# Attention's second score product and the mLSTM's g product over 128 partitions in place of 64

## The chip, the core and the metric

The kernel runs on one core of a Trainium2 chip. The metric is device time in microseconds (us) of one execution. The core has TensorE (PE, with its weight loader PEld), VectorE (DVE), ScalarE (ACT) and GpSimd (POOL), which take their instructions in an order of their own each and wait for each other by semaphores; SyncE (SP) issues the DMAs.

## What is computed

Two layers, each of a mixer and a feed-forward block, on 512 tokens of 1024 features, with a norm ahead of and behind each block. The mixer has eight heads of dilated attention (64 features each) and four heads of an mLSTM (128 features each, two directions, chunks of 128 tokens):

```python
def reference(x, ...):
    for l in range(DEPTH):                       # 2
        mixed = hybrid_mixer(rms_norm(x, mix_pre_g[l]), w_in[l], ..., w_out[l])
        x = x + rms_norm(mixed, mix_post_g[l])
        ff = conv_ffn(rms_norm(x, ffn_pre_g[l]), w_up[l], ..., w_down[l])
        x = x + rms_norm(ff, ffn_post_g[l])
...
        # one step of a direction of the mLSTM, for one chunk
        inter = bcum + m_st[..., None]
        m_t = jnp.maximum(inter, jnp.max(dlog, axis=-1))
        sc = jnp.einsum('bhte,bhse->bhts', qc, kc) * jnp.exp(dlog - m_t[..., None])
        g = jnp.exp(inter - m_t)
        num = jnp.einsum('bhts,bhsf->bhtf', sc, vc) + g[..., None] * jnp.einsum('bhte,bhef->bhtf', qc, c_st)
```

## The kernel before

Activations lie in SBUF with the feature on the partition and the 512 tokens along the row. Each float32 operand of a projection is split into a high and a low part, and a product is made of three: high by high, low weight by high, high weight by low (`mac`, L200 to L202). The weights come in 192 pieces of at most 512 KB over SP's queue into three raw buffers; ACT makes the high part of a piece (L153) and DVE the low part (L91).

In the mixer the projections run through PE in a written order, and the side work of the heads is put between them: `Stream` A steps through the generators `attn`, and `Stream` M through `gates` and `mlstm`, a step after so many tiles of products. A planner then fixes the order of each engine's instructions when the program is made, by priorities, by the costs that it assumes and by the points that `issue_after` sets. Work of the norms is due after a certain number of rows of products (`later`, `settle`).

*Attention scores.* `rot_out` turns the queries and keys of two heads, a and b, in one tile of 128 partitions (a in rows 0 to 63, b in rows 64 to 127). Of the queries it makes one tile per head, with the head's high part in its own 64 rows and the low part in the other 64. Of the keys it makes one tile per head with the high part twice (`ak0`, `ak1`), and one tile `ak2` with the low parts of both heads. In `scores` L710 makes low and high query by high key in one product over 128 partitions, and L711 adds high query by low key, over the head's own 64 partitions. DVE then adds a bias and takes the minimum (L716), ACT makes the exponentials (L719) and scales them (L721), `turn` transposes on PE (L727) and makes two parts (L730 on ACT, L91 on DVE), and L753 multiplies by the values. There are 32 score tiles in a layer.

*The mLSTM.* `gates` makes `bdm` and `bdg`, rows that hold -M and m_prev - M of a chunk as high and low parts in partitions 0 to 63, and in `bdm` also an indicator of the chunk in partitions 64 to 127. `uu` holds ones in partitions 0 to 63 and the parts of u in 64 to 127; `lu` is `uu` with the rows of other heads and directions set to nothing. L812 multiplies `lu` by `bdm` over 128 partitions, L820 multiplies the first 64 rows of `lu` by those of `bdg`; ACT makes the exponential of each (L814, L822). There are eight products of either line in a layer.

Buffers come from pools by tag; a new tile on a tag waits until the readers of the last one are through. The mixer's pool and the feed-forward block's lie over the same space, one after the other.

Of the kernel before, what the change touches and what calls it, by code (L numbers as in the profile page):

```python
# [9 lines left out]
F32R = mybir.dt.float32r  # L10
# [4 lines left out]
PSUM = bass.MemoryType.PSUM  # L15

P = 128
T = 512
D = 1024
KT = D // P  # L20
# [12 lines left out]
# per head: the order of its projections (mLSTM q and k, both values, attention q and k), and its attention's rate  # L33
# [3 lines left out]
# columns of the per-feature parameter array  # L37
# [8 lines left out]
# columns of the constant array  # L46
# [12 lines left out]
def tile_hybrid_block(ctx: ExitStack, tc: tile.TileContext, xt, w_in, w_g, w_out, w_up, w_down, par, cst, out):  # L59
    nc = tc.nc  # L60
# [77 lines left out]
    def split_w(alloc=None):  # L138
        """the next piece as exact high and low parts; alloc gives their place, n of the eight rows at a time."""
        if not raw_q:  # L140
            return None
        raw, nk = raw_q.popleft()
        parts = {}
        n = 8
        k = 0
        while k < nk:
            if alloc is None:
                hi = whi_p.tile([P, 8, P], F32R, tag="whi", name="whi")
                lo = wlo_p.tile([P, 8, P], F32R, tag="wlo", name="wlo")
            else:  # L150
                hi, lo, n = alloc()
            m = min(n, nk - k)
            nc.scalar.copy(out=hi[:, 0:m, :], in_=raw[:, k:k + m, :])  # L153
            lo_part(lo[:, 0:m, :], raw[:, k:k + m, :], hi[:, 0:m, :])
            for j in range(m):
                parts[k + j] = (hi[:, j, :], lo[:, j, :])
            parts["all"] = (hi, lo)
            k += m
        load_raw()
        return parts  # L160
# [18 lines left out]
    # work to be put into the program once the tensor engine has so many more rows of products before it  # L179
# [12 lines left out]
    def mac(ps, w, kk, rhs, first, last, cols=None):  # L192
        """ps += w[:, kk, :]^T rhs with both operands as exact high and low parts."""
        settle()
        clock[0] += 3 * (T if cols is None else cols.stop - cols.start)
        hi, lo = w[kk]
        rh, rl = rhs
        if cols is not None:
            rh, rl = rh[:, cols], rl[:, cols]
        nc.tensor.matmul(out=ps, lhsT=hi, rhs=rh, start=first, stop=False)  # L200
        nc.tensor.matmul(out=ps, lhsT=lo, rhs=rh, start=False, stop=False)  # L201
        clock[1] = nc.tensor.matmul(out=ps, lhsT=hi, rhs=rl, start=False, stop=last).ins  # L202

# [1 line left out]
    class Stream:  # L205
        """generators one after another, a step at a time behind the products that come before it."""
# [29 lines left out]
    def rsqrt(ms, n):  # L236
        """1/sqrt(ms) on [P, n], by a first guess from the exponent and Newton steps."""
        y = sm.tile([P, n], F32, tag=f"rs_y{n}", name="rs_y")
        a = sm.tile([P, n], F32, tag=f"rs_a{n}", name="rs_a")
        yi = y[:, :].bitcast(I32)  # L240
        nc.vector.tensor_scalar(yi, ms.bitcast(I32), -0.5, float(0x5F3759DF), op0=ALU.mult, op1=ALU.add)
        for _ in range(3):
            nc.vector.tensor_tensor(out=a, in0=y, in1=y, op=ALU.mult)
            nc.vector.scalar_tensor_tensor(out=a, in0=a, scalar=-0.5, in1=ms, op0=ALU.mult, op1=ALU.mult)
            nc.vector.scalar_tensor_tensor(out=y, in0=a, scalar=1.5, in1=y, op0=ALU.add, op1=ALU.mult)
        return y

    def rsqrt_cols(ms):
        """for the two columns of ms [P, 2]: RS / sqrt(ms), by a first guess from the exponent and Newton steps."""
# [9 lines left out]
        # a third-order step, a = y^2 ms within 7% of 1: (a^2 + C1 a + C0) y = s / sqrt(ms)  # L259
# [4 lines left out]
        # Newton's: (y^2 ms - 3 s^2) y = -2 s^3 / sqrt(ms)  # L264
# [7 lines left out]
    class Stats:  # L272
        """Sums of squares over the features: the first tiles add up beside the tensor engine, which sums over the
        partitions of that sum and of each of the last `own` tiles."""
# [7 lines left out]
        def add(self, src, n, hf):  # L282
            """the n-th of the KT tiles, for the tokens of one half or (None) both."""
# [17 lines left out]
        def flush(self, h):  # L301
            """what has come for a half until now, the sum of the first tiles ahead."""
            if self.sp[h] is None:
                self.sp[h] = t_ps()
                nc.vector.memset(self.sp[h][:, 0:2], EPS)
                self.sums(h, 1, self.acc[:, halves[h]])
            for g, n, sq in self.late:
                if g == h:
                    self.sums(h, n - KT + self.own + 2, sq)
            self.late = [e for e in self.late if e[0] != h]  # L310
# [6 lines left out]
        def rstd(self, hf):  # L317
            """[P, 2] for a half, a token per partition."""
# [6 lines left out]
    def row_of(r):  # L325
        """[P, 2] with a token per partition -> [P, 256] PSUM with the token along the row, in every partition."""
# [11 lines left out]
    def pre_operand(g, k, ops, st, hf):  # L338
        """x * g as parts, and the square of x into the statistics."""
        parts_of(g, k, ops, hf)  # L340
        st.add(x[k][:, slice(0, T) if hf is None else halves[hf]], k, hf)
# [29 lines left out]
    class Post:  # L371
        """x += norm(m) * g for each half of the tokens, and the next block's operand from the new x."""
# [9 lines left out]
        def put(self, k, src, cols=slice(0, T)):  # L382
            """an output tile times the norm's gain."""
# [30 lines left out]
    def first_group(ws, pss, xp, scale, extra=None):  # L414
        """the tiles whose operand is still being made: by halves of the tokens, all tiles beside each other."""
# [10 lines left out]
    def last_tiles(ws, kts, act, post, n0, also=None):  # L426
        """the last output tiles by halves of the tokens, so that the norm of the first half overlaps the second."""
# [18 lines left out]
    def mixer_first(l, xp, sp, G, more, whole=False):  # L446
# [12 lines left out]
        if whole:  # L459
            # the input comes tile by tile  # L460
# [20 lines left out]
    def mixer(l, xp, first, mp, post):  # L481
# [10 lines left out]
        # what picks a direction's and head's own rows for the decay products: the chunk's m and, below, the chunk  # L492
# [18 lines left out]
        def gates(ps):  # L511
# [14 lines left out]
            # index: direction, step, head; the backward direction's step j is chunk 3 - j  # L526
# [6 lines left out]
            # log sigmoid(f) = min(f, 0) - log1p(exp(-|f|)), the log1p as 2 atanh(e / (2 + e))  # L533
# [32 lines left out]
            # running maxima, forward for the first 16 rows and backward for the others  # L566
# [19 lines left out]
            # the state's maximum before each step, and with the step's own  # L586
# [16 lines left out]
            # keys are twice their value until here, and carry the scale  # L603
# [3 lines left out]
            # rows: -M and m_prev - M in the chunk's own columns, as parts  # L607
# [8 lines left out]
            bdg = mp.tile([P, 4, P], F32R, tag="bdg", name="bdg")  # L616
            for bd, src, place in ((bdm, nm, "Q0"), (bdg, gm, "Q1")):
# [12 lines left out]
        def conv_out(ps, i, name):  # L630
            """five taps, then twice the silu."""
# [15 lines left out]
        def v_out(pss):  # L647
            """values of both kinds with the token on partitions: [P, chunk, kind, feature], two chunks in a bank."""
# [22 lines left out]
        def rot_out(ps, name):  # L671
# [12 lines left out]
            if name == "aq":  # L684
                # a head's high and low parts on top of each other
# [3 lines left out]
            else:  # L689
                # a head's high part twice, and the low parts of both heads  # L690
                lo = mp.tile([P, T], F32R, tag="ak2", name="ak2")
                nc.scalar.copy(out=t[0][B_], in_=f32v(t[0][A_]))
                nc.scalar.copy(out=t[1][A_], in_=f32v(t[1][B_]))
                lo_part(lo[A_], a[A_], t[0][A_])
                lo_part(lo[B_], a[B_], t[1][B_])
                st[name] = (t, lo)
# [5 lines left out]
        def attn(hp):  # L702
# [3 lines left out]
            def scores(a, qt):  # L706
                r = slice(64 * a, 64 * a + 64)
# [3 lines left out]
                nc.tensor.matmul(out=s, lhsT=qs2[a][r, qs], rhs=kl[r, :], start=False, stop=True)  # L711
                p_ = mp.tile([P, T], F32, tag="p", bufs=2, name="p")
                mx = sm.tile([P, 1], F32, tag="mx", bufs=4, name="mx")
                # -(s + bias) / 8 and its minimum
# [46 lines left out]
        def mlstm(h):  # L761
# [3 lines left out]
            # keys with the token on partitions, times what enters the state  # L765
# [32 lines left out]
            # the part that each direction sees  # L798
# [8 lines left out]
            for d in range(2):  # L807
# [7 lines left out]
                # the masked half may overflow, and is nothing in sm_  # L815
# [4 lines left out]
                nc.tensor.matmul(out=gp_, lhsT=lu[0:64, :], rhs=st["bdg"][0:64].rearrange("p c t -> p (c t)"), start=True, stop=True)  # L820
# [38 lines left out]
        # projections; side work of the heads goes between them  # L859
# [3 lines left out]
        # streams of side work, each with its steps for each part of a projection tile  # L863
# [15 lines left out]
        def proj_v():  # L879
            """the tokens as the output's rows: both kinds of values beside each other."""  # L880
# [49 lines left out]
        # output projection  # L930
# [179 lines left out]
    # loads in the order in which the first products need them  # L1110
# [42 lines left out]
def _constants():  # L1153
# [32 lines left out]
    # how many of the dilated patterns hold key - query, as a bias before the scale  # L1186
# [63 lines left out]
```

## Time and profile before

| | |
|---|---|
| time, median of 3 runs | 1391.45 us (1390.81 to 1391.57) |
| span of the profiled execution | 1389.7 us; what lies around it has no record of its own, and the median stands 1.75 us above it |
| PE busy | 1359.0 us, 98%, 7152 products |
| PEld busy | 1126.2 us, 81% |
| DVE busy | 955.7 us, 69% |
| ACT busy | 721.8 us, 52% |
| POOL busy | 105.9 us, 8% |
| DMA | 115.34 MB, 83 GB/s |

A line such as L711 is a line of the kernel. In a shape, `64*128 64x512` is a left operand of 64 partitions by 128 columns and a right one of 64 by 512. PE's products overlap: the end of one is modelled, and a busy share near 1 says that some product was always under way, not how many were finished. A view of the timeline gives the start and the duration of each; one of windows gives the busy time of each engine in a stretch, the number of instructions, PE's granted clock (1.00 is 2.4 GHz, half of that is 1.2) and the DMAs' share and rate.

### The profile page before, as it was taken

The numbers are of one execution on the slowest core, as the hardware profiler recorded it, in microseconds if no ns is written. First come the engines' busy times: TensorE is split into PE (matmuls) and PEld (weight loads), VectorE is DVE, ScalarE is ACT, GpSimd is POOL, SyncE is SP. The second block draws the span as 40 slices with busy tenths as digits, with TensorE's granted clock in tenths as the row PEclk, the third lists the DMA queues.
The fourth block names the chain that finished last, engine by engine and source line by source line (L and its number), as shares of the span: only waits on it lengthen the run. The fifth ranks groups of instructions, "written<-read, shape, count | busy, mean of one in ns | idle before, by whom it ended". The sixth has DMA issues, their size and how long they took to land. (4 is left out here: it accounts for less than half of the span.)

```text
span 1389.7 us, 18680 instructions
## 1 busy us (share of the span) xinstructions
PE 1359.0 (98%) x7152; PEld 1126.2 (81%) x7152; DVE 955.7 (69%) x1885; ACT 721.8 (52%) x1226; POOL 105.9 (8%) x110
## 2 busy tenths in 40 slices
PE   7999999999999999999999999999999999999997
PEld 6778878789888888888986888787898888888886
DVE  6989788747887777422498887778479777773233
ACT  5686686754544444323356766866546444442230
POOL 0000000024000000000120000000240000000102
PEclk9999999999999999999999999999999999999999
DMA  6212122140333333233311121122412333323221
GB/s 231 61 35 88 31 61 77 48 150 2 100 98 107 91 95 99 86 96 103 99 67 61 61 61 51 42 77 74 124 47 76 107 91 96 102 87 99 90 89 61
DMA packets 34089, 115.34 MB, mean 83 GB/s; under 512 B 3664, under 2 KB 6352, under 8 KB 34000
## 3 DMA queue, kind: packets, MB, share of 16 engines
q1 hardware_dynamic: 34000, 114.15, 27.0%
q8 instruction: 56, 0.92, 0.3%
q14 instruction: 33, 0.27, 0.1%
HBM read 112.04 MB, written 2.10 MB: 82 GB/s over the span
## 5 line engine op out<-in xcount | busy, mean ns | idle before, releaser
L91 DVE TENSOR_TENSOR wlo<-wraw,whi 128x1024 fp32r<-128x1024 f32 (+1 forms) x192 | 236.5, 1234 | 180.6 <-ACT whi L153 178.8
L200 PE MATMUL mm<-ah,whi 128*128 128x512 f32 (+1 forms) x880 | 342.0, 389 | 0.0
L201 PE MATMUL mm<-ah,wlo 128*128 128x512 f32 (+1 forms) x880 | 335.3, 381 | 0.0
L202 PE MATMUL mm<-al,whi 128*128 128x512 f32 (+1 forms) x880 | 334.1, 381 | 0.9 <-DVE al L348 0.8
L153 ACT CAST whi<-wraw 128x1024 fp32r<-128x1024 f32 (+1 forms) x192 | 197.6, 1034 | 168.6 <-PE mm L202 112.4
L200 PEld LDWEIGHTS mm<-ah,whi 128*128 128x128 f32 x880 | 166.5, 189 | 39.1 <-issue 12.0
L202 PEld LDWEIGHTS mm<-al,whi 128*128 128x128 f32 x880 | 166.2, 189 | 32.3 <-issue 1.9
L201 PEld LDWEIGHTS mm<-ah,wlo 128*128 128x128 f32 x880 | 166.6, 189 | 27.8 <-issue 1.9
L296 POOL TENSOR_TENSOR acc<-acc,sq 128x512 f32<-128x512 f32 x22 | 29.6, 1345 | 764.1 <-ACT sq L293 759.8
L200 PE MATMUL mm<-hh,whi 128*128 128x512 f32 x220 | 86.7, 394 | 0.0
L201 PE MATMUL mm<-hh,wlo 128*128 128x512 f32 x220 | 86.7, 394 | 0.0
L202 PE MATMUL mm<-hl,whi 128*128 128x512 f32 x220 | 86.7, 394 | 0.0
L1029 DVE TENSOR_TENSOR u<-mm,prow 128x512 f32<-128x512 f32 x64 | 43.8, 686 | 50.1 <-PE mm L202 39.6
L893 PE MATMUL mm<-whi,ah 128*128 128x256 f32 x256 | 74.4, 292 | 0.2 <-DVE cu L633 0.2
L1046 ACT CAST hh<-cv 128x512 fp32r<-128x512 f32 x44 | 27.3, 620 | 87.5 <-DVE cv L1043 87.5
L895 PE MATMUL mm<-whi,al 128*128 128x256 f32 x256 | 72.4, 283 | 0.0
L894 PE MATMUL mm<-wlo,ah 128*128 128x256 f32 x256 | 72.4, 283 | 0.0
L1041 ACT ACTIVATE cg<-cg 128x512 f32<-128x512 f32 x44 | 27.9, 633 | 74.5 <-DVE cg L1035 74.2
L201 PE MATMUL o<-ah,wlo 128*128 128x512 f32 (+1 forms) x160 | 60.6, 379 | 0.0
L200 PE MATMUL o<-ah,whi 128*128 128x512 f32 (+1 forms) x160 | 60.5, 378 | 0.0
L202 PE MATMUL o<-al,whi 128*128 128x512 f32 (+1 forms) x160 | 60.5, 378 | 0.0
L719 ACT ACTIVATE p<-p,mx 128x512 f32<-128x512 f32 x64 | 46.1, 720 | 21.6 <-DVE mx L716 21.6
(317 smaller groups left out, 2788.3 us busy)
## 6 DMA issues: line engine op xcount, KB each, us to landing
wraw<-in_w_up SPq DMA_DIRECT2D x88, 512.0 KB, 3.6
wraw<-in_w_in SPq DMA_DIRECT2D x56, 512.0 KB, 3.5
wraw<-in_w_down SPq DMA_DIRECT2D x32, 512.0 KB, 3.5
wraw<-in_w_out SPq DMA_DIRECT2D x16, 512.0 KB, 3.5
wraw<-in_w_down SPq DMA_DIRECT2D x16, 384.0 KB, 3.1
x<-in_xt SPq DMA_DIRECT2D x4, 512.0 KB, 7.3
out_dram<-x SPq DMA_DIRECT2D x8, 256.0 KB, 2.2
tb<-in_cst SPq DMA_DIRECT2D x2, 967.0 KB, 5.1
```

The costliest lines, as they stand in the source:

```text
L91: nc.vector.tensor_tensor(out=dst, in0=src, in1=f32v(hi), op=ALU.subtract)
L153: nc.scalar.copy(out=hi[:, 0:m, :], in_=raw[:, k:k + m, :])
L200: nc.tensor.matmul(out=ps, lhsT=hi, rhs=rh, start=first, stop=False)
L201: nc.tensor.matmul(out=ps, lhsT=lo, rhs=rh, start=False, stop=False)
L202: clock[1] = nc.tensor.matmul(out=ps, lhsT=hi, rhs=rl, start=False, stop=last).ins
L296: e.tensor_tensor(out=self.acc[:, cols], in0=self.acc[:, cols], in1=sq, op=ALU.add)
L719: nc.scalar.activation(out=p_, in_=p_, func=AF.Exp, scale=-1.0, bias=mx, accum_out=den)
L893: nc.tensor.matmul(out=o_, lhsT=xh, rhs=hi, start=(k == 0), stop=False)
L894: nc.tensor.matmul(out=o_, lhsT=xh, rhs=lo, start=False, stop=False)
L895: clock[1] = nc.tensor.matmul(out=o_, lhsT=xl, rhs=hi, start=False, stop=(k == KT - 1)).ins
L1029: nc.vector.tensor_tensor(out=u, in0=ps, in1=st["row"], op=ALU.mult)
L1041: nc.scalar.activation(out=g, in_=g, func=AF.Gelu_apprx_tanh)
```

## The change

The second score product takes all 128 rows of the query's tile, and a key tile of its own for each head, `klo[0]` or `klo[1]`, which holds the low part in the head's own rows and zeros in the other 64. The zeros are written once in a layer by two memsets on POOL, and the two tiles live as long as the mixer. `bdg` gets zeros in partitions 64 to 127 by a memset on POOL, and L820 takes all 128 rows of `lu` and `bdg`. The space that the program keeps free for DMA descriptors is set to 1024 bytes of a partition. Apart from this the diff takes out comments and docstrings, and leaves their lines empty.

```diff
@@ gates
             bdg = mp.tile([P, 4, P], F32R, tag="bdg", name="bdg")
+            nc.gpsimd.memset(f32v(bdg[64:128]), 0.0)
@@ rot_out
-                lo = mp.tile([P, T], F32R, tag="ak2", name="ak2")
                 nc.scalar.copy(out=t[0][B_], in_=f32v(t[0][A_]))
                 nc.scalar.copy(out=t[1][A_], in_=f32v(t[1][B_]))
-                lo_part(lo[A_], a[A_], t[0][A_])
-                lo_part(lo[B_], a[B_], t[1][B_])
-                st[name] = (t, lo)
+                lo_part(klo[0][A_], a[A_], t[0][A_])
+                lo_part(klo[1][B_], a[B_], t[1][B_])
+                st[name] = (t, klo)
+
+        klo = [mp.tile([P, T], F32R, name=f"klo{i}") for i in range(2)]
+        nc.gpsimd.memset(f32v(klo[0][64:128]), 0.0)
+        nc.gpsimd.memset(f32v(klo[1][0:64]), 0.0)
@@ attn, scores
-                r = slice(64 * a, 64 * a + 64)
                 qs = slice(qt * P, (qt + 1) * P)
                 s = s_ps()
                 nc.tensor.matmul(out=s, lhsT=qs2[a][:, qs], rhs=kh[a], start=True, stop=False)
-                nc.tensor.matmul(out=s, lhsT=qs2[a][r, qs], rhs=kl[r, :], start=False, stop=True)
+                nc.tensor.matmul(out=s, lhsT=qs2[a][:, qs], rhs=kl[a], start=False, stop=True)
@@ mlstm
-                nc.tensor.matmul(out=gp_, lhsT=lu[0:64, :], rhs=st["bdg"][0:64].rearrange("p c t -> p (c t)"), start=True, stop=True)
+                nc.tensor.matmul(out=gp_, lhsT=lu, rhs=st["bdg"].rearrange("p c t -> p (c t)"), start=True, stop=True)
@@ kernel
-    nc = bacc.Bacc("TRN2", target_bir_lowering=False, num_devices=1)
+    nc = bacc.Bacc("TRN2", target_bir_lowering=False, num_devices=1, dynamic_dma_scratch_size=1024)
```

## Rows read from the trace of the kernel before

**Rows 1.** The page: each engine's busy time, share of the span, instructions.

```profile
PE 1359.0 (98%) x7152; PEld 1126.2 (81%) x7152; DVE 955.7 (69%) x1885; ACT 721.8 (52%) x1226; POOL 105.9 (8%) x110
```

**Rows 2.** Windows of the first mixer: length, engines' busy time (instructions), clock, DMA.

```profile
60.00:100.00 40.00, 39.31 (x195) 28.84 (x195) 33.90 (x88) 32.90 (x65) 0.00 (x0) 1.00 0.14 40
100.00:140.00 40.00, 40.00 (x260) 34.27 (x259) 37.03 (x81) 26.95 (x52) 2.90 (x2) 1.00 0.27 80
140.00:180.00 40.00, 39.64 (x241) 33.30 (x241) 31.42 (x79) 25.44 (x52) 3.44 (x2) 1.00 0.13 40
180.00:220.00 40.00, 39.13 (x215) 30.18 (x214) 32.91 (x87) 35.16 (x70) 0.00 (x0) 1.00 0.18 52
220.00:265.00 45.00, 45.00 (x253) 35.44 (x252) 35.02 (x73) 29.91 (x57) 2.59 (x2) 1.00 0.23 68
```

**Rows 3.** Groups by line and shape: count, busy us, mean ns, idle before.

```profile
L711 PE MATMUL s<-ak,aq 64*128 64x512 f32 x64 | 31.7, 495 | 0.0
...
L820 PE MATMUL s<-bdg,lu 64*128 64x512 f32 x16 | 8.0, 498 | 0.0
...
L812 PE MATMUL s<-bdm,lu 128*128 128x512 f32 x16 | 6.5, 406 | 0.0
```

**Rows 4.** Timeline of PE around one second score product: start, duration, instruction.

```profile
202.91 0.39 PE L202 MATMUL mm<-al,whi 128*128 128x512 f32 x1
203.14 0.40 PE L710 MATMUL s<-ak,aq 128*128 128x512 f32 x1
203.46 0.50 PE L711 MATMUL s<-ak,aq 64*128 64x512 f32 x1
203.89 0.50 PE L200 MATMUL mm<-ah,whi 128*128 128x512 f32 x1
204.23 0.28 PE L753 MATMUL o<-ptl,vs 128*128 128x256 f32 x1
```

**Rows 5.** Chain that ended last, second mixer: start, us on the chain, instruction.

```profile
869.83 0.43 PE s L711
...
890.83 0.23 PE s L710
891.07 0.43 PE s L711
891.49 0.43 PE mm L200
...
892.98 0.69 DVE p L716
...
950.44 0.42 PE s L711
```

**Rows 6.** Waits of PE's weight loader: what for, us in all, times, longest.

```profile
PEld s L711 <- issue: 18.3, 64, 0.4
```

**Rows 7.** Windows of L711's products alone: length, PE busy (count), clock, DMA.

```profile
60.00:100.00 40.00, 3.96 (x8) 1.00 0.14 40
100.00:140.00 40.00, 2.48 (x5) 1.00 0.27 80
140.00:180.00 40.00, 1.48 (x3) 1.00 0.13 40
180.00:220.00 40.00, 3.97 (x8) 1.00 0.18 52
220.00:265.00 45.00, 3.96 (x8) 1.00 0.23 68
```

**Rows 8.** Window of L820's products alone in the first mixer.

```profile
60.00:265.00 205.00, 3.98 (x8) 1.00 0.19 56
```

**Rows 9.** Groups of POOL by line and shape: a memset.

```profile
L104 POOL MEMSET ones<- 128x128 f32 x1 | 0.2, 204 | 0.3 <-POOLq L1237 0.3
```

**Rows 10.** Windows at the border of the two layers, columns as in rows 2.

```profile
690.00:700.00 10.00, 7.79 (x62) 6.74 (x61) 9.70 (x24) 5.37 (x14) 6.04 (x8) 1.00 0.00 1
700.00:710.00 10.00, 9.87 (x72) 9.22 (x71) 9.59 (x22) 5.60 (x14) 6.10 (x9) 0.83 0.03 5
```

## The prediction, made before the changed kernel was run

> **What bounds the kernel now.** I read the engines' totals first, then the windows by stretch, then the products by shape, and last the timeline of TensorE (PE) and the chain of work that ended last, around the products that change.
>
> The totals [rows 1] show one engine that is nearly always occupied: PE, 98% of the span, with VectorE (DVE) at 69% and ScalarE (ACT) at 52%. A busy PE need not be a fast one, because the ends of pipelined products are modelled; what counts is the time from the start of one product to the start of the next. So the share alone doesn't say that a product costs more than it must.
>
> The products that change all lie in the two mixers. The first mixer's side work runs from 60 to 265 us, and the second repeats it from 745 to 955 us. In the first one [rows 2] PE is busy for 39.13 to 45.00 us of stretches of 40 to 45 us at the full granted clock (1.00). The reader is to see the two engines behind it as well: DVE is at 37.03 of 40 us in the densest stretch (0.926), and ACT reaches 35.16 of 40 (0.88) at 180 to 220 us. Below I use this 0.926 as the fullest that a helper engine has been seen in these stretches while PE stood still for nothing (40.00 of 40).
>
> **What a 64-row product costs.** There are 64 products on L711 and 16 on L820 [rows 3]; the shape column says 64 partitions in place of 128, and their mean is 495 and 498 ns, against 406 for L812, which writes the same kind of tile with the same 512 columns, but over 128 partitions. Durations overlap, so the price is read from starts. On the timeline [rows 4], L202 starts at 202.91 and L710 at 203.14, 0.23 us later: that is the step of full-height products of 512 columns. Then the 64-row product starts at 203.46, L200 at 203.89 and L753 at 204.23. From 202.91 to 204.23 are 1.32 us for four products of 512 columns; four steps of 0.23 are 0.92. So one 64-row product among full-height ones costs 1.32 - 0.92 = 0.40 us more than a full-height one would in its place: 0.09 before it, 0.20 in its own step and 0.11 in the step of the product behind it.
>
> The chain of work says the same in another way [rows 5]. L710 ahead of a 64-row product is on it with 0.23 us, L711 with 0.43, and the L200 behind it with 0.43 as well: 2 x 0.43 - 2 x 0.23 = 0.40. A third sign is the weight load. PE's loader sat idle for 18.3 us in all ahead of the 64 loads of L711, for no reason that the profile shows [rows 6]: 0.29 us each. So a 64-row load is not made beneath the product ahead of it, which the even step of 0.23 between full-height ones needs.
>
> **The change part by part.** (1) L711 takes all 128 rows of the query's tile and of a key tile with 64 rows of zeros: 64 products. (2) L820 takes all 128 rows of `lu` and of `bdg`: 16 products. The trace of before has no such product with zeros in it. The nearest row is L812, full height, 512 columns and the same `lu`; I take its kind's step, 0.23. That gives 80 x 0.40 = 32.0 us less PE time, 16.0 us in each mixer. The bounds of this term are 0 (zeros over 128 rows cost what 64 rows cost, a rival below) and 32.0.
>
> (3) Not all of this is on the path. From 853 us on, the chain [rows 5] holds 18 of the 20 64-row products that the trace has there (the first and the last of the 18 are shown); it misses those beside which the chain runs through DVE and ACT, as from 892.98 on. At 18 of 20, 32.0 becomes 28.8 us.
>
> (4) A faster PE asks for the helpers' results sooner. Say that no helper may be fuller than 0.926 in any stretch, with nothing borrowed from the neighbours. The stretches of [rows 2] can then shrink to 33.90 / 0.926 = 36.6, 40.0, 33.9, 38.0 (ACT) and 37.8 us, which is by 3.4, 0, 6.1, 2.0 and 7.2 us. The 64-row products of L711 in them are 8, 5, 3, 8 and 8 [rows 7], worth 3.2, 2.0, 1.2, 3.2 and 3.2 us at 0.40. The smaller of the two, stretch by stretch, is 3.2 + 0 + 1.2 + 2.0 + 3.2 = 9.6 of 12.8 us: 75%. The eight products of L820 in this mixer [rows 8] I let go the same way, and so the second mixer: 0.75 x 32.0 = 24.0 us. This is too strict, since split weights and scores are made ahead and a late one can be caught up in the next stretch; 28.8 is too kind, since it lets no new wait arise. I take the middle, 26.4.
>
> (5) The zeros are written by three memsets on GpSimd (POOL) in each mixer, of 64 x 512, six in all. POOL's memset of 128 x 128 took 0.204 us [rows 9]. One of 64 x 512 has four times the columns, so I bound it by 0.2 and 0.8 us. For four of the six POOL has time: it is busy for 105.9 us of the span [rows 1] and not at all at 60 to 100 us [rows 2]. The two for the keys' low parts in the second mixer may fall where POOL adds into x and sums squares at the border of the layers, 700 to 710 us, with 6.10 of 10 us busy [rows 10]. The next norm waits for those. With this cover gone they cost at most 2 x 0.8 = 1.6 us, and nothing if they are queued behind; I take 0.
>
> (6) The low parts of the keys go to two tiles in place of one, with the same two DVE subtractions of 64 rows: no price. What grows is the space, a tile of 512 columns more; to make room, the bytes set aside for descriptors are cut. The page lists only the hardware queue and the instructions' own, and no DMA appears in the terms above, so I price this at 0. If tiles of the mixer now lie over others of the feed-forward block, a first write at a border waits for another reader. The cover is again that one border at 690 to 720 us.
>
> Sum: the execution profiled spans 1389.7 us, 1.75 under the median of 1391.45, and this difference I keep. 1389.7 - 26.4 = 1363.3, or 1365.0 against the median.
>
> **The rivals.** *The helpers hold the pace (0.19).* The time saved comes back as waits of PE for DVE and ACT wherever one of them is over 0.8 now. Then only 140 to 180 and 220 to 265 us give anything: 1.2 + 3.2 = 4.4 of 12.8, or 34% of 32.0 = 11.0 us, 1380.4 us. For it speaks that the chain leaves PE for DVE at 892.98; against it, that PE waits for nothing beside a DVE at 0.926.
>
> *A product's height doesn't matter (0.05).* The 0.40 would then belong to the place of these products in the order of work, and would stay: 1391.5 us. Against it, L820 and L711 stand in different places and cost the same, and L812, a neighbour of L820, is 90 ns shorter. The Trainium skill has this rule, in "TensorE: Matmul & The Clock Gate", section "Why this matters for your kernels": a single product with a small contraction takes as long as a full one, and only several side by side in the array gain. By that rule the sum would be 0; the trace here doesn't agree, with 0.43 against 0.23 us for a step.
>
> *More than I sum (0.04).* All 80 are on the path and some of PE's other waits shrink: a saving of more than 34 us, under 1357.
>
> *Slower (0.04).* PE runs ahead of DVE, stands idle, and its clock falls. At 690 to 700 us PE was idle for 2.2 us, and in the 10 us after it the granted clock was 0.83 [rows 10]: 3.4 us at 1.2 GHz in place of 2.4, so 1.7 us of work lost, 3.9 us in all for one such event. Against 26.4 us, seven of them would cancel the change, and eleven would end 16 us above it, at 1408. Against it speaks a granted clock of 1.00 in all five stretches [rows 2], DVE at 0.926 included.
>
> **How the numbers follow.** My forecast has the remaining chance, 0.68, and its own range is the savings from 20 to 34 us, 1357 to 1371. Above lies the helpers' rival, up to some 1384. The range 1356 to 1382 leaves out its upper tail (0.03), the two cases of no gain (0.09) and a little below (0.03), 0.15 in all. No change means within 0.2%, 2.8 us, about what a measurement of this kernel can tell. Faster 0.68 + 0.19 + 0.04 = 0.91, the same 0.05, slower 0.04.
>
> **What would show it.** In the profile after, L711 and L820 read 128 x 512 with a mean near 400 ns, the steps around them on the timeline are 0.23, and the loader's idle time ahead of L711 is gone. The mixers end some 13 us earlier each, while the feed-forward blocks take what they took. The prediction is wrong in its first term if L711's neighbours still step by 0.43, and in its fourth if the steps are 0.23 but PE waits for DVE or ACT in the stretches by more than about 4 us a mixer, or if the order of the work on the engines has changed so that the same waits come elsewhere.

## The result, and the profile after

The changed kernel takes 1365.93 us against 1391.48 (medians of 4 runs each), 0.9818 of the time before, with a 95% interval of 0.9804 to 0.9831: 25.5 us less. The forecast was 1365.0. The profiled execution spans 1364.3 us, 25.4 less than before.

The page after, its first part, answers to [rows 1]. PE is busy for 29.8 us less. The others are busy about as long as before, POOL for 3.5 us more, of which six memsets of 0.52 us are 3.1:

```profile
span 1364.3 us, 18689 instructions
...
PE 1329.2 (97%) x7152; PEld 1127.2 (83%) x7152; DVE 955.4 (70%) x1885; ACT 719.4 (53%) x1226; POOL 109.4 (8%) x116
```

Lines moved with the diff: L711 is now L714, L710 L713, L820 L823 and L812 L815. The groups by shape after, against [rows 3]:

```profile
L714 PE MATMUL s<-klo,aq 128*128 128x512 f32 x64 | 25.3, 396 | 0.0
...
L823 PE MATMUL s<-bdg,lu 128*128 128x512 f32 x16 | 6.5, 409 | 0.0
```

They read 128 partitions, and their means fell from 495 and 498 to 396 and 409 ns. On the timeline of PE after, against [rows 4], every step is 0.23 us, into, over and out of the second product:

```profile
194.25 0.39 PE L202 MATMUL mm<-al,whi 128*128 128x512 f32 x1
194.48 0.39 PE L713 MATMUL s<-ak,aq 128*128 128x512 f32 x1
194.71 0.40 PE L714 MATMUL s<-klo,aq 128*128 128x512 f32 x1
194.94 0.39 PE L200 MATMUL mm<-ah,whi 128*128 128x512 f32 x1
195.17 0.63 PE L756 MATMUL o<-ptl,vs 128*128 128x256 f32 x4
```

From the first to the last of them are 0.92 us where the same five took 1.32 before. The view of waits after lists no unexplained idle time of the loader ahead of L714 (18.3 us ahead of L711 in [rows 6]). The windows of the first mixer after, against [rows 2], show fuller helpers:

```profile
60.00:100.00 40.00, 39.32 (x227) 32.50 (x227) 37.10 (x96) 36.08 (x71) 0.00 (x0) 1.00 0.15 42
100.00:140.00 40.00, 39.45 (x272) 36.06 (x272) 37.95 (x84) 25.23 (x49) 3.15 (x2) 1.00 0.25 78
140.00:180.00 40.00, 38.60 (x225) 32.53 (x223) 33.12 (x81) 30.00 (x61) 3.45 (x2) 1.00 0.18 53
180.00:220.00 40.00, 39.72 (x261) 34.66 (x260) 33.80 (x86) 33.14 (x64) 0.00 (x0) 1.00 0.18 54
220.00:265.00 45.00, 45.00 (x254) 38.15 (x253) 37.82 (x94) 33.27 (x73) 2.59 (x2) 1.00 0.24 72
```

From 100 to 140 us DVE is at 37.95 of 40 us now (0.949), and from 60 to 100 us ACT is at 36.08 (0.90). Where the mixers end is seen from the first use of a feed-forward product, in the view of a line (its x32: durations, first and last start). Before, L1029 had it; the same line of the changed kernel, for either layer:

```profile
L1032 DVE TENSOR_TENSOR u<-mm,prow x32: 678/691/692, 344.4 to 552.8; 128x512 f32<-128x512 f32 x32
...
L1032 DVE TENSOR_TENSOR u<-mm,prow x32: 681/684/692, 1019.5 to 1227.8; 128x512 f32<-128x512 f32 x32
```

The same view of the kernel before reads 357.6 and 1044.9 us. So the first mixer is 13.2 us shorter, all of 25.4 us is there by the second one's end, and from the first to the last start of this line the feed-forward blocks take 208.4 and 208.3 us, where both took 208.4 before.

### The profile page after: what moved, and what is told of

Its sections match the earlier page's. It is cut to its first block, busy times and chain, and to the rows that moved or that the text cites. A ratio compares the mean times of both kernels' runs of the same rounds, so it can differ in the third digit from the quotient of the medians.

```text
span 1364.3 us, 18689 instructions
## 1 busy us (share of the span) xinstructions
PE 1329.2 (97%) x7152; PEld 1127.2 (83%) x7152; DVE 955.4 (70%) x1885; ACT 719.4 (53%) x1226; POOL 109.4 (8%) x116
## 5 line engine op out<-in xcount | busy, mean ns | idle before, releaser
L200 PE MATMUL mm<-ah,whi 128*128 128x512 f32 (+1 forms) x880 | 336.4, 383 | 0.0
```

## The experiments

All ratios are to the kernel before, on the same chip, with their 95% intervals. Each edit is shown against the changed kernel.

**All but the height.** Both products over 64 partitions, everything else as changed.

```diff
-                nc.tensor.matmul(out=s, lhsT=qs2[a][:, qs], rhs=kl[a], start=False, stop=True)
+                nc.tensor.matmul(out=s, lhsT=qs2[a][slice(64 * a, 64 * a + 64), qs], rhs=kl[a][slice(64 * a, 64 * a + 64)], start=False, stop=True)
...
-                nc.tensor.matmul(out=gp_, lhsT=lu, rhs=st["bdg"].rearrange("p c t -> p (c t)"), start=True, stop=True)
+                nc.tensor.matmul(out=gp_, lhsT=lu[0:64, :], rhs=st["bdg"][0:64].rearrange("p c t -> p (c t)"), start=True, stop=True)
```

> Everything of the change but the height: two key tiles, six memsets, the smaller space for descriptors, but both products over 64 partitions as before. My theory (the whole gain is the height of the 80 products, the room and the memsets cost nothing): 1391.5 us, within 1 us of the kernel before. Rival (the new places of the tiles or the memsets at the border of the layers cost or give something): 1 to 3 us off, either way.

Measured: 1392.19 us, 1.0004 (0.9994 to 1.0013). By the times, the two key tiles, the six memsets and the room cost nothing that can be told. This kernel, the changed one and the one before have the same order of work on PE, DVE and ACT, and on POOL but for the memsets and one sum that trades places with a small memset, so that the traces can be set side by side, start by start. They show a small cost of the memsets after all. From 20 us on, PE in this kernel runs level with the one before, within 0.1 us, until the border of the layers, and it is some 0.5 us behind from there to the end. In the kernel before, from the timelines of POOL, ACT and PE:

```profile
711.26 0.74 POOL L404 TENSOR_TENSOR x<-x,fg 128x256 f32<-128x256 f32 x1 [0.89 <-DVE rs_y L262]
712.04 0.51 ACT L347 ACTIVATE ah<-x,par 128x256 fp32r<-128x256 f32 x1 [2.55 <-POOL x L404]
712.60 0.31 PE L454 MATMUL mm<-ah,wg 128*32 128x256 f32 x1 [0.42 <-ACT ah L347]
```

And in this kernel:

```profile
711.29 0.52 POOL L617 MEMSET bdg<- 64x512 f32 x1
711.89 0.72 POOL L404 TENSOR_TENSOR x<-x,fg 128x256 f32<-128x256 f32 x1
712.64 0.51 ACT L347 ACTIVATE ah<-x,par 128x256 fp32r<-128x256 f32 x1 [3.07 <-POOL x L404]
713.20 0.31 PE L454 MATMUL mm<-ah,wg 128*32 128x256 f32 x1 [1.13 <-ACT ah L347]
```

POOL's addition into x stands behind the memsets of the border (the last of them is shown) and starts 0.63 us later; ACT waits for it, and PE for ACT.

**The parts alone.** One of the two edits above, each.

> The 64 second score products over 128 partitions, the 16 g products over 64. Theory (0.40 us of PE time for each half-height product, some 0.32 us of it reaching the end): 64/80 of the 25.5 us, 20.4 us, 1371.1 us. Rival (the places decide, and the g products stand where PE sets the pace while many score products do not): a gain of 15 us or less.

> The 16 g products over 128 partitions, the 64 second score products over 64. Theory: 16/80 of 25.5 us, 5.1 us, 1386.4 us, and with the run above the two parts add up to the whole. Rival (each part is worth more alone, since PE then has less to wait for): the two gains add up to 28 us or more.

Measured: the scores alone 1369.14 us, 0.9841 (0.9826 to 0.9855); g alone 1386.78 us, 0.9966 (0.9954 to 0.9978). That is 22.1 and 4.7 us by the ratios, 26.9 together, against 25.3 for the whole. The rival of 15 us or less from the scores falls. The two parts add up to the whole within the intervals, which are some 2 us wide to either side for each part; so wide, they don't exclude the 28 us of the other rival, that each part is worth a little more alone.

**Pairs of half-height products.** Both products of a score tile over 64 partitions, and g too, by the edit of the first experiment.

```diff
-                nc.tensor.matmul(out=s, lhsT=qs2[a][:, qs], rhs=kh[a], start=True, stop=False)
-                nc.tensor.matmul(out=s, lhsT=qs2[a][:, qs], rhs=kl[a], start=False, stop=True)
+                nc.tensor.matmul(out=s, lhsT=qs2[a][slice(64 * a, 64 * a + 64), qs], rhs=kh[a][slice(64 * a, 64 * a + 64)], start=True, stop=False)
+                nc.tensor.matmul(out=s, lhsT=qs2[a][slice(64 * a, 64 * a + 64), qs], rhs=kl[a][slice(64 * a, 64 * a + 64)], start=False, stop=True)
```

> Both products of a score tile over the head's own 64 partitions, the g products over 64 too; the first product so leaves out the queries' low part by the keys' high part. There are 64 half-height products more, each next to another half-height one. Theory (the price lies in the passage from full to half height and back, so a pair costs as much as one): the time of the run without the height, 1391.5 us, within 3 us; on the timeline the second product of a pair follows after 0.23 us. Rival (each half-height product costs 0.40 us, whatever stands next to it): 64 x 0.40 = 25.6 us more PE time, 1412 to 1417 us.

Measured: 1390.07 us, 0.9990 (0.9980 to 0.9999). There are 64 half-height products more, and no time is added. PE's timeline in this kernel:

```profile
201.81 0.39 PE L202 MATMUL mm<-al,whi 128*128 128x512 f32 x1
202.13 0.50 PE L713 MATMUL s<-ak,aq 64*128 64x512 f32 x1
202.47 0.39 PE L714 MATMUL s<-klo,aq 64*128 64x512 f32 x1
202.79 0.51 PE L200 MATMUL mm<-ah,whi 128*128 128x512 f32 x1
203.14 0.63 PE L756 MATMUL o<-ptl,vs 128*128 128x256 f32 x4
```

The four steps are 0.32, 0.34, 0.32 and 0.35 us, 1.33 in all, as with the one half-height product of [rows 4]. Over all 64 second products the medians of the step into them, of their own and of the one behind are 0.34, 0.32 and 0.34 us. Against 0.23, the two steps into half height are 0.20 us longer together here, and the two out of it 0.21. So the price is not paid for a half-height product, but for the passage to half height and back, some 0.2 us each way. One detail of the expectation was off: the second of a pair starts 0.34 us after the first, not 0.23, because the records split a passage over the step ahead of it and its own. The loader says the same. With all but the height it sat idle for no shown reason ahead of all 64 loads of the second product; in this kernel it does so ahead of 4, and 4 is also the number of second products that stand behind a full-height one here:

```profile
PEld s L714 <- issue: 1.1, 4, 0.4
```

Two things differ here beside the height: the first product no longer needs the copies of the key into the other 64 rows, and two of the pairs of each mixer are taken apart by the planner, their first products next to each other and then their second ones. The kernel takes 2.1 us less than the one with all but the height, and part of that may come from these; they can't hide 25.6 us.

**More passages.** The kernel with all but the height, and the W product over 64 rows as well.

```diff
-                nc.tensor.matmul(out=ep, lhsT=lu, rhs=st["bdm"].rearrange("p c t -> p (c t)"), start=True, stop=True)
+                nc.tensor.matmul(out=ep, lhsT=lu[0:64, :], rhs=st["bdm"][0:64].rearrange("p c t -> p (c t)"), start=True, stop=True)
```

> The kernel with the room but without the height, and 16 more half-height products: the W product over 64 partitions too, which leaves out u in its exponent. They stand alone among full-height ones, 8 in each mixer; the order of every engine is the same. Theory (a lone half-height product costs 0.40 us of PE time, and in the slower state of before PE sets the pace, so that nearly all of it reaches the end): 16 x 0.40 = 6.4 us, 5 to 6.5 us above the run without the height, 1397 to 1399 us. Rival (the helpers hold the pace in the mixers, so PE time there is worth little): under 3 us, below 1395.

Measured: 1396.87 us, 1.0033 (1.0020 to 1.0045). By the medians, each against the kernel before on its own chip, that is 4.4 us more than with all but the height, for 6.4 offered; the intervals leave this difference some 2 us to either side. Start by start the two traces differ by 2.2 us in each mixer, for 3.2 offered, so 0.7 of the PE time reaches the end. That is less than I wrote and more than the rival.

**Less PE time still.** The changed kernel without its second score product, and beside it the changed kernel itself.

```diff
-                nc.tensor.matmul(out=s, lhsT=qs2[a][:, qs], rhs=kh[a], start=True, stop=False)
-                nc.tensor.matmul(out=s, lhsT=qs2[a][:, qs], rhs=kl[a], start=False, stop=True)
+                nc.tensor.matmul(out=s, lhsT=qs2[a][:, qs], rhs=kh[a], start=True, stop=True)
```

> The changed kernel itself, timed on the chip of the runs beside it: 1366 us.

> The changed kernel without the second score product, so without the queries' high part by the keys' low part: 64 full-height products of 0.23 us, 14.7 us of PE time, are gone. Theory (some 0.8 of PE time saved in the mixers reaches the end, here as well): 11.8 us, 1354 us. Rival (from here the helpers hold the pace, and the next PE time saved is worth much less): under 6 us, above 1360 us. The planner may order the engines' work in another way, since instructions are gone.

Measured: the changed kernel on this chip 1366.47 us, 0.9818 (0.9805 to 0.9832); without the product 1355.08, 0.9734 (0.9721 to 0.9748). That is 11.4 us of 14.7, or 0.78, and the rival of under 6 us falls. PE still sets the pace of the mixers after the change, much as it did before. The planner's order differs here, and the first product waits for less, so the 0.78 is a rough one.

**Three attempts at what came back.** In the first, the g product goes to a buffer of the transposes. In the second, GpSimd makes two copies that ACT made. In the third, the memsets take the whole of the two key tiles and DVE has less to do.

```diff
-                gp_ = s_ps()
+                gp_ = t_ps()
```

> The changed kernel, with the g product written to a buffer of the transposes in place of one of the two score buffers. Theory (of the 32 us, some 6.5 come back as waits of PE for helpers, and the largest of them is the W product's, for the score buffer that ACT's exponential of g still reads): 1 to 2 us faster than the changed kernel, 1364 to 1365 us. Rival (the wait moves to the transposes, or comes from elsewhere): the time of the changed kernel or more.

```diff
-                nc.scalar.copy(out=t[0][B_], in_=f32v(t[0][A_]))
-                nc.scalar.copy(out=t[1][A_], in_=f32v(t[1][B_]))
+                nc.gpsimd.tensor_copy(out=t[0][B_], in_=f32v(t[0][A_]))
+                nc.gpsimd.tensor_copy(out=t[1][A_], in_=f32v(t[1][B_]))
```

> The changed kernel, with the two copies of the keys' high part into the other 64 rows made by GpSimd in place of ACT. Theory (part of what PE won comes back where the first score product of a head waits for these copies at the end of ACT's queue, 1.1 us once in each mixer): 0.5 to 1.5 us for each mixer, 1363.5 to 1365.5 us. Rival (GpSimd's copy takes over 1.3 us, as its additions of twice the rows do, and comes later than ACT's): the time of the changed kernel or 1 to 3 us more.

```diff
-                lo_part(klo[0][A_], a[A_], t[0][A_])
-                lo_part(klo[1][B_], a[B_], t[1][B_])
...
-        nc.gpsimd.memset(f32v(klo[0][64:128]), 0.0)
-        nc.gpsimd.memset(f32v(klo[1][0:64]), 0.0)
+        nc.gpsimd.memset(f32v(klo[0][:]), 0.0)
+        nc.gpsimd.memset(f32v(klo[1][:]), 0.0)
```

> The changed kernel without the 16 subtractions on DVE that make the keys' low parts (the low parts stay zero): 16 x 0.69 = 11 us less DVE work in the mixers, the same PE work. Theory (what came back of the 32 us are waits for ACT and DVE as they stand in their queues, and DVE's load is a good part of it): 1 to 4 us less, 1362 to 1365 us. Rival (the waits hang on ACT or on the order of the work, and DVE's load on nothing that PE waits for): under 1 us. The planner may order the work in another way, since instructions are gone.

Measured, in this order: 1369.10 us, 0.9834 (0.9821 to 0.9848); 1367.17 us, 0.9820 (0.9805 to 0.9834); 1371.47 us, 0.9852 (0.9835 to 0.9868). None beats the changed kernel. With g in a buffer of the transposes, PE no longer waits for ACT's exponential of g ahead of the W product (1.1 us in the changed kernel), but its waits for ACT ahead of the transposes of the scores grow from 0.6 to 1.6 us: the wait moved, as the rival has it. With GpSimd's copies the first score product does start earlier, but PE waits there for 1.00 us all the same (1.12 before this edit). This is the product in that kernel's timeline:

```profile
173.85 0.60 POOL L692 CAST ak<-ak 64x512 fp32r<-64x512 f32 x1 [9.17 <-ACT ak L683]
174.51 0.30 PEld L713 LDWEIGHTS s<-ak,aq 128*128 128x128 f32 x2 [1.42 <-POOL ak L692]
174.51 0.73 PE L713 MATMUL s<-ak,aq 128*128 128x512 f32 x2 [1.00 <-POOL ak L692]
```

The kernel without the subtractions, which were 10.9 us, keeps DVE busy for 8.0 us less and takes 5 us more. The planner had ordered its engines' work in another way, as it did in the first one and, in fewer places, in the second. So none of the three says what its single wait or DVE's load is worth. That the 5 us come from the order is likely, but no run here shows it by itself.

**Products over 32 partitions.** The gates' small products over 128 partitions, their operands in tiles of 128 partitions that a memset zeroes first.

```diff
-                nc.tensor.transpose(gp[:, c * 32:(c + 1) * 32], gs[:, c * P:(c + 1) * P], ident[0:32, 0:32])
+                nc.tensor.matmul(out=gp[:, c * 32:(c + 1) * 32], lhsT=gs[:, c * P:(c + 1) * P], rhs=ident[:, 0:32], start=True, stop=True)
...
-            nc.tensor.matmul(out=cp[:, 0:32], lhsT=ones[0:32, :], rhs=dgm, start=True, stop=True)
-            nc.tensor.transpose(cp[:, 32:64], cm, ident[0:32, 0:32])
+            nc.tensor.matmul(out=cp[:, 0:32], lhsT=ones, rhs=dgmf, start=True, stop=True)
+            nc.tensor.matmul(out=cp[:, 32:64], lhsT=cmf, rhs=ident[:, 0:32], start=True, stop=True)
```

> The changed kernel, with the 14 products of the gates over 32 partitions made over 128, with zeros in the rest (the transposes among them as products with a part of the identity). Theory (a passage to a lower height and back costs, 0.2 to 0.4 us for each of six groups of such products): 1 to 2 us less, 1364 to 1365 us. Rival (the products over 32 partitions stand where PE waits for the gates' vector work anyway, or their own step of 0.06 us is worth as much): within 1 us of the changed kernel.

Measured: 1367.59 us, 0.9825 (0.9811 to 0.9840), no gain. The run doesn't tell what a passage to 32 rows costs, because the edit makes more products: the trace holds 24 in place of 14, two for each transpose. For the eight transposes of the gates' inputs, in the changed kernel and then in this one:

```profile
L516 PE MATMUL t<-c,gs 32*128 32x32 f32 x8 | 0.9, 228 | 0.0
...
L516 PE MATMUL t<-c,gs 128*128 128x32 f32 x16 | 2.0, 260 | 0.0
```

From the product ahead of four of them to the second one behind are 0.92 us in the changed kernel, in the second layer, and 1.13 here. Of the two places, only the other (L582) stands where PE waits for the gates' vector work, 0.7 us in each layer. The planner's order differs here as well.

## Why the prediction was right, step by step

**The price of a product.** The steps gave 0.40 us for each of 80 products, and the changed kernel shows the same five starts 0.40 us closer. The price holds for all 80: start by start, from the kernel with all but the height to the changed one, the steps that shrank add up to 16.0 us in the first mixer and 15.8 in the second, where the prediction has 16.0 for each. The prediction named a load that isn't made beneath the product ahead; the pairs add that this hangs on the change of height, not on the 64 rows. The rival that a product's height doesn't matter falls with the runs: the kernel with all but the height takes 1392 us, the whole 1366. For the half-height products themselves the rival's rule holds: the four steps of the pair are 1.33 us, less one price of 0.40 this leaves 0.93, so 0.23 for each of the four, the half-height two among them. This is what the Trainium skill says in "TensorE: Matmul & The Clock Gate", section "Why this matters for your kernels": a single product with a small contraction takes as long as a full one. Another page of the Trainium skill bears on the price, "TensorEngine Tiling (Array Packing)", section "Key Properties": changing the tiling mode, not just the tile, drains the engine. The trace agrees in so far as the price stands at the change, some 0.2 us each way; that a drain makes it is not shown by any run here.

**Of 32.0 us, 25.5 arrive: 0.80.** The prediction took the middle, 26.4, between 28.8 (the share on the chain) and 24.0 (no helper fuller than 0.926). That the result lies so near the middle is in part luck, since nothing but the two bounds spoke for it. The lower bound was right in kind and too strict. Start by start, the five stretches of the first mixer gave back 3.5, 1.8, 1.5, 2.2 and 3.7 us of the 4.0, 2.8, 1.6, 3.6 and 4.0 that their 64-row products offered, L820's included. So the two in which a helper was fullest gave the smallest shares, 0.66 and 0.62, as the fourth term has it; but it let nothing arrive from 100 to 140 us, and DVE went on to 0.949. The upper bound took the loss for products that lie off the chain. The traces show it as waits: in either mixer 19 steps grew by 0.05 us or more, 2.9 us together. In the first mixer, which the second repeats, two steps grew most. They are shown here first in the kernel with all but the height, then in the changed one:

```profile
137.39 0.28 PE L898 MATMUL mm<-whi,al 128*128 128x256 f32 x1
137.50 0.39 PE L815 MATMUL s<-bdm,lu 128*128 128x512 f32 x1
...
180.72 0.39 PE L202 MATMUL mm<-al,whi 128*128 128x512 f32 x1
181.82 0.51 PE L713 MATMUL s<-ak,aq 128*128 128x512 f32 x1 [0.71 <-ACT ak L692]
```

```profile
131.19 0.28 PE L898 MATMUL mm<-whi,al 128*128 128x256 f32 x1
132.00 0.50 PE L815 MATMUL s<-bdm,lu 128*128 128x512 f32 x1 [0.54 <-ACT Q L825]
...
173.58 0.39 PE L202 MATMUL mm<-al,whi 128*128 128x512 f32 x1
175.08 0.50 PE L713 MATMUL s<-ak,aq 128*128 128x512 f32 x1 [1.12 <-ACT ak L692]
```

L815 used to follow after 0.11 us and now after 0.81, because the score buffer is still read by ACT's exponential of g. L713 followed after 1.10 us and now after 1.50, because PE comes to it 7.1 us sooner and ACT's copy of the key lets it start only 6.7 us sooner. That is 1.1 us a mixer; a little more lies in nine steps that grew by 0.1 to 0.3 us, most of them ahead of transposes and value products, whose inputs ACT and DVE make, and the rest in eight smaller ones. The two largest waits are for ACT, which is busy for 0.63 and 0.75 of the stretches in which they stand; so they are waits for single results that come late in a queue, not for an engine that is full. Ahead of L713, ACT itself waits for DVE before it makes the key's high parts and their copies:

```profile
173.13 0.62 ACT L683 CAST ak<-ra 64x512 fp32r<-64x512 f32 x1 [1.39 <-DVE ra L680]
```

So the sum closes: of 32.0 us, 5.8 come back as such waits and 0.5 at the border of the layers, where the memsets stand. That these waits cause the loss is read from the traces; the attempts to take single ones away didn't gain, and so don't prove it.

**The memsets** were taken at 0, and cost some 0.5 us, inside the bounds of 0 and 1.6. They took 0.52 us each, inside the bounds of 0.2 and 0.8, and two of them did fall at the border of the layers, ahead of a sum of squares; so did the one for `bdg`, which the prediction did not count there and which stands ahead of the addition into x. POOL's timeline of the changed kernel there:

```profile
696.17 0.52 POOL L699 MEMSET klo<- 64x512 f32 x1
696.74 0.52 POOL L700 MEMSET klo<- 64x512 f32 x1
697.23 0.73 POOL L296 TENSOR_TENSOR acc<-acc,sqq 128x256 f32<-128x256 f32 x1
```

**The rivals.** The helpers don't hold the pace: their rival had 11.0 us, 25.5 came, and some 0.78 of the next 14.7 us arrived too. More than the sum, over 34 us, did not come either. Nor did the slower rival: the granted clock is 1.00 in the five stretches shown, DVE at 0.949 included.

## What to carry to other kernels

Read the price of a product from the starts of its neighbours too, not from its duration: 0.20 of the 0.40 us here stood in the steps before and behind it. Where PE sets the pace, a lone product over half of the rows among full-height ones is worth filling up with zeros; where it can't be filled, put such products next to each other, since a pair added no time over a half-height product among full ones. Of PE time saved or added in these mixers, where the helpers are at 0.8 to 0.95, 0.7 to 0.8 reached the end, and the rest went into small waits for single results. Look also at what a cheap memset stands ahead of on its engine.

## What the runs showed of the hardware beside this

A left operand that is narrow, and not short, shows no such price here. In the changed kernel's timeline a gate product of 128 x 16 steps as its full-width neighbours do:

```profile
17.86 0.39 PE L202 MATMUL mm<-al,whi 128*128 128x512 f32 x1
18.08 0.40 PE L456 MATMUL mm<-al,wg 128*16 128x512 f32 x1
18.32 0.39 PE L200 MATMUL mm<-ah,whi 128*128 128x512 f32 x1
```

Here 0.22 and 0.24 us stand on either side of it.

The clock at the border of the layers differs between executions of much the same work. It was granted at 0.83 from 700 to 710 us before [rows 10], and at 1.00 in the same place of the changed kernel, after the same wait of PE for 1.98 us. It was 1.00 there in a second profiled execution of the changed kernel too, while the kernel with all but the height fell to half of it at 700 us, like the one before. This difference has no part in the 25.5 us. At the lower clock PE falls 1.5 us behind by 705 us, start by start, and is level again by 710, because at the full clock PE waits there for DVE (a step of 0.90 us ahead of L456, where the lower clock has 0.12). The prediction's price of 3.9 us for such an event was too high at this place. The timeline's row of the wait of 1.98 us and the window behind it, in the changed kernel:

```profile
686.21 0.71 PE L329 MATMUL s<-ident_rs,rs_y 128*128 128x128 f32 x4 [1.98 <-DVE rs_y L266]
```

```profile
686.00:696.00 10.00, 9.04 (x72) 8.01 (x72) 9.60 (x22) 5.23 (x14) 5.69 (x8) 1.00 0.01 2
```
